# Merge gates and branch products by rows of tokens with transposed merged rows, and a hand-ordered tail in smaller pieces

## The chip, the core and the metric

One core of a Trainium2 chip runs the kernel alone. The metric is device microseconds (us) of one execution; the time before is 429.8 us, the median of three runs (429.72 to 430.73). The engines are TensorE (PE; its weight loads are listed apart as PEld), VectorE (DVE), ScalarE (ACT), GpSimd (POOL) and SyncE (SP), which here issues the loads of the weights and the stores of the output.

## The reference, cut to what matters

One decoder layer on 256 tokens of width 1024. Three attention mixers give `o_a`, `o_b` and `o_c` (together 1024 wide). Each is projected to 1024, the three are merged by sigmoid gates, and the merged rows go through `w_out`. A gated feed-forward part and a last RMS norm follow.

```python
gates = sigmoid(mg).reshape(b, s, 3, 1024)             # mg: 3072 columns of norm(x) @ w_in
merged = (gates[:, :, 0] * (o_a @ wb[:r0]) + gates[:, :, 1] * (o_b @ wb[r0:r1])
          + gates[:, :, 2] * (o_c @ wb[r1:]))
x = x + merged @ w_out
x = x + conv_ffn(rmsnorm(x, norm_ffn), w_up, conv_w, conv_b, w_down)
return rmsnorm(x, norm_final)
```

## The kernel before

All is float32. To keep its precision, each operand of the large products is cut into a high and a low part, and `mm3` (L239) makes three products of each: low by high, high by low, high by high. So one "product" of the mathematics is three instructions of TensorE, each with its own weight load.

**Weights.** `_unit_list` (L69) cuts all weights into units, most of 1 MB (2048 floats for each of 128 partitions), which SyncE loads in the order in which the program asks for them into `raw` buffers (4, and a fifth once the attention's memory is free). ACT copies a unit into its high part `whi` (L224), DVE subtracts to get the low part `wlo` (L228), each in two halves of 1024 floats. There are 2 buffers for such pairs, and 5 once the attention is done; a unit keeps its pair until its last product has been made.

**Order.** Outside of blocks marked `manual_schedule`, Tile's planner orders each engine's instructions ahead of time: what comes first in the program has priority, and where that isn't ready, something later that is ready is put in its place. On the chip each engine then keeps this order. PSUM tiles of a pool are taken when free: `psg` and, after the attention, `psg2` have two banks each, and `psa` has the four banks of the sums `acc[t][n]` (t: half of the tokens, n: half of the 1024 columns).

**Gates and branches, before.** Everything is computed transposed, with 128 output channels on the partitions and the 256 tokens along the free axis. `gates(i)` (L668) takes three units (one for each branch) of 256 gate columns; for each of two chunks of 128 columns `chunk_T` (L343) makes 24 instructions with the weights as the stationary operand and the 256 tokens moving, and ACT copies the 128x256 result into `gl`. There are 12 such units, i.e. 24 chunks and 576 instructions. The first two calls follow the attention in the program, so that their products are put into its holes; the other two are in the merge loop. The loop over four quarters of the columns (L725) loads `br{i}` and `wo{i}`, takes the sigmoid, and for each chunk makes the three branch products (9, 9 and 6 instructions with 256 moving columns), which DVE multiplies by the gates and adds up (L748 to L751) into `mg`. `mg` is already the transposed form that the product with `w_out` needs as its stationary operand; it is cut into `mh` (ACT, L754) and `ml` (DVE, L755).

`later` (L706) holds the products with `w_out` back: a chunk's 12 instructions of 512 columns are put in the program one chunk later (two at the end), so that TensorE need not wait for `mh` and `ml`. What is still held at the end is given out by `flush(t, n)` in the hand-ordered block that follows (L827), in which the sums are added to `x`, squared, transposed (L784) and split for the feed-forward part.

**The tail, before** (L946 to L960). The planner orders it. For each half t of the tokens: the last three chunks' products of the down projection, 9 instructions for each `acc[t][n]`; two adds of 512 columns, each followed by a sum of squares on ACT (L169); the rest of the norm (L178 on DVE, the power on POOL, L180); a product with the norm's weights (L953); a scaling of one half of the columns on DVE (L957) and one on ACT (L959); and two stores of 256 KB by SyncE (L960).

## Time and profile before

| | before |
|---|---|
| median of 3 runs | 429.80 us |
| the profiled execution | 429.01 us |
| span of its instructions | 427.2 us |
| TensorE busy | 417.7 us (98%) |
| DVE busy | 309.6 us (72%) |
| ACT busy | 253.6 us (59%) |
| mean granted TensorE clock | 0.995 |

The span runs from the first instruction to the last; the profiled execution took 1.8 us more than its span. A TensorE instruction's listed duration includes its passage through the array, which overlaps the next instruction's, so what a stream of products costs is the distance between the starts of two neighbours. The trace has three stages that matter here: the attention, until about 127 us; gates, branches and the product with `w_out`, from 127 to 234 us; and the tail, from about 413 us.

### The profile page before, as it was taken

The page shows a single profiled execution, that of the slowest core. Times are in us where ns is not written, and L with a number is a line of the kernel's source. Part 1 is how long each engine was busy: PE and PEld are TensorE (multiplying, and loading weights), DVE is VectorE, ACT ScalarE, POOL GpSimd, SP SyncE. Part 2 cuts the span into 40 slices and gives each one's busy share as a digit, 9 for nine tenths or more (in the row PEclk, how much of TensorE's full clock was granted, in tenths as well). Part 3 has the DMA queues.
Part 4 walks back from the last instruction along what each step waited for, and adds up shares of the span by engine and source line. Part 5 has one row for each costly group of instructions (what it writes and reads, how often), then busy time and mean ns, then how long its engine had stood idle before and what let it go on. Part 6 is the DMA issues. An engine that isn't in the chain of part 4 may idle for free.

```text
span 427.2 us, 7237 instructions
## 1 busy us (share of the span) xinstructions
PE 417.7 (98%) x2848; PEld 373.8 (87%) x2848; DVE 309.6 (72%) x641; ACT 253.6 (59%) x463; POOL 13.1 (3%) x19
## 2 busy tenths in 40 slices
PE   9999999999999999999999999999999999999993
PEld 8998888987779998999998998988888888888882
DVE  5756753798864697539345899998797797887764
ACT  6443282458787774445345889567576575584633
POOL 4201000000000000000000100000000000000001
PEclk9999999999999999999999999999999999999997
DMA  8988719532209785544540274665753743700002
GB/s 303 394 352 300 266 51 342 202 125 83 100 2 334 281 329 189 198 163 153 195 179 2 100 294 162 234 216 197 277 202 103 288 176 120 295 2 0 2 0 98
DMA packets 12609, 78.05 MB, mean 183 GB/s; under 512 B 1392, under 2 KB 1408, under 8 KB 4640
## 3 DMA queue, kind: packets, MB, share of 16 engines
q1 hardware_dynamic: 12000, 75.48, 47.5%
q0 software_dynamic: 576, 2.12, 1.6%
q8 instruction: 22, 0.36, 0.3%
q14 instruction: 11, 0.09, 0.1%
HBM read 76.52 MB, written 1.07 MB: 182 GB/s over the span
## 4 chain that ended last, share of the span: by engine, by line
PE 89%; ACT 4%; DVE 4%; issue 2%; POOL 0%; POOLq 0%; ACTq 0%
PE g L240 14%; PE g L242 13%; PE g L241 13%; PE g L924 12%; PE g L926 6%; PE acc L240 6%; PE acc L241 6%; PE acc L242 6%; PE o L489 2%; PE t L470 2%; PE g L824 2%; PE g L289 1%; PE s L456 1%; DVE cy L903 1%; PE g L882 1%
## 5 line engine op out<-in xcount | busy, mean ns | idle before, releaser
L228 DVE TENSOR_TENSOR wlo<-raw,whi 128x1024 fp32r<-128x1024 f32 (+2 forms) x130 | 153.9, 1204 | 48.4 <-ACT whi L224 47.7
L224 ACT ACTIVATE whi<-raw 128x1024 fp32r<-128x1024 f32 (+2 forms) x130 | 129.9, 1039 | 35.9 <-PE g L242 23.2
L240 PE MATMUL g<-hn_hi,wlo 128*128 128x256 f32 x376 | 108.2, 288 | 0.1
L241 PE MATMUL g<-hn_lo,whi 128*128 128x256 f32 x376 | 107.5, 286 | 0.0
L242 PE MATMUL g<-hn_hi,whi 128*128 128x256 f32 x376 | 107.2, 285 | 0.0
L924 PE MATMUL g<-parts,whi 128*128 128x512 f32 x256 | 89.4, 396 | 0.0
L240 PEld LDWEIGHTS g<-hn_hi,wlo 128*128 128x128 f32 x376 | 72.0, 191 | 2.9 <-issue 1.4
L242 PEld LDWEIGHTS g<-hn_hi,whi 128*128 128x128 f32 x376 | 72.0, 192 | 1.1 <-issue 1.0
L241 PEld LDWEIGHTS g<-hn_lo,whi 128*128 128x128 f32 x376 | 72.0, 192 | 0.7 <-issue 0.5
L926 PE MATMUL g<-parts,wlo 128*128 128x256 f32 x256 | 66.2, 279 | 0.0
L924 PEld LDWEIGHTS g<-parts,whi 128*128 128x128 f32 x256 | 46.7, 188 | 9.2
L926 PEld LDWEIGHTS g<-parts,wlo 128*128 128x128 f32 x256 | 48.2, 188 | 2.8
L903 DVE SCALAR_TENSOR_TENSOR cy<-xn,small_b,cy 128x255 f32<-128x255 f32 (+1 forms) x88 | 41.4, 478 | 8.9 <-ACT cy L901 8.0
L240 PE MATMUL acc<-whi,fl 128*128 128x512 f32 x88 | 34.5, 392 | 0.1
L241 PE MATMUL acc<-wlo,fh 128*128 128x512 f32 x88 | 34.3, 390 | 0.0
L242 PE MATMUL acc<-whi,fh 128*128 128x512 f32 x88 | 34.2, 389 | 0.0
L901 ACT ACTIVATE cy<-xn,small_b 128x256 f32<-128x256 f32 x44 | 25.8, 598 | 7.4 <-DVE xn L933 7.4
L932 ACT ACTIVATE xn<-g 128x256 f32<-128x256 f32 x32 | 12.2, 380 | 22.2 <-PE g L924 22.2
L674 ACT ACTIVATE gl<-g 128x256 f32<-128x256 f32 x24 | 9.1, 378 | 21.7 <-PE g L242 21.7
L242 PEld LDWEIGHTS acc<-whi,fh 128*128 128x128 f32 x88 | 16.5, 188 | 3.6
L933 DVE TENSOR_TENSOR xn<-g,xn 128x256 f32<-128x256 f32 x32 | 13.4, 420 | 8.4 <-ACT xn L932 8.4
L241 PEld LDWEIGHTS acc<-wlo,fh 128*128 128x128 f32 x88 | 16.5, 188 | 3.3
(190 smaller groups left out, 589.6 us busy)
## 6 DMA issues: line engine op xcount, KB each, us to landing
raw<-in_wts_dram SPq DMA_DIRECT2D x62, 1024.0 KB, 4.9
gl<-in_w_dram SPq DMA_DIRECT2D x8, 512.0 KB, 7.1
raw<-in_wts_dram SPq DMA_DIRECT2D x2, 804.0 KB, 7.5
raw<-in_wts_dram SPq DMA_DIRECT2D x3, 512.0 KB, 6.7
T<-tvd POOLq DMA_DIRECT2D x1, 1280.0 KB, 13.5
xs<-in_x_dram SPq DMA_DIRECT2D x2, 516.0 KB, 3.7
out_dram<-raw SPq DMA_DIRECT2D x4, 256.0 KB, 2.2
T<-tvd POOLq DMA_DIRECT2D x1, 768.0 KB, 7.7
```

What stands on the lines that cost most here:

```text
L224: nc.scalar.activation(self.parts[0][:, sl], self.raw[:, sl], AF.Copy)
L228: return (eng or nc.vector).tensor_sub(self.parts[1][:, sl], self.raw[:, sl], self.parts[0][:, sl].bitcast(F32))
L240: nc.tensor.matmul(ps, al, bh, start=start, stop=False)
L241: nc.tensor.matmul(ps, ah, bl, start=False, stop=False)
L242: nc.tensor.matmul(ps, ah, bh, start=False, stop=stop)
L674: nc.scalar.activation(gl[c][:, b, :], chunk_T(plain(u, c)), AF.Copy)
L901: on_act.append(nc.scalar.activation(y, u, AF.Identity, bias=vec_c[:, 3, ch:ch + 1], scale=vec_c[:, 2, ch:ch + 1]))
L903: nc.vector.scalar_tensor_tensor(y[:, sh:], u[:, :S - sh], vec_c[:, w, ch:ch + 1], y[:, sh:], op0=ALU.mult, op1=ALU.add)
L924: hi = lambda: nc.tensor.matmul(ps, u[0][:, k, cols], h_parts[:, k].rearrange("p a q -> p (a q)"), start=k == 0, stop=k == KC - 1)
L926: lo = lambda: nc.tensor.matmul(ps[:, :S], u[1][:, k, cols], h_parts[:, k, 0, :], start=False, stop=False)
L932: nc.scalar.activation(part, ps[:, S:], AF.Copy)
L933: nc.vector.tensor_add(v, ps[:, :S], part)
```

## The change

Gates and branch products are made by rows: 128 tokens on the partitions and 512 columns along the free axis. The activations become the stationary operand and the weights the moving one. The gates come from 12 units again, but each holds 512 rows by 512 columns; `by_rows` (the body of the former `proj_V`) makes 12 instructions of 512 columns for each half of the tokens and each unit, 288 in all. The branch products become 96 instructions of 512 columns in place of 192 of 256. They use `psg` alone, and the second half's gates use `psg2`. The merge runs in two halves of 512 columns in place of four quarters. The gates of one branch of a half are a tile of 128x1024, on which the sigmoid is taken at once; DVE multiplies in place and adds into `mg`, which now has tokens on the partitions. So 16 transposes on TensorE are new: eight per half, four into each bank. `mh` and `ml` are made from that bank, 128x512 at a time. The products with `w_out` are held back four chunks.

The tail gets a hand-written order. The last block of the sums, `acc[1][1]`, is given out as twice 9 instructions of 256 columns, the second of them into a bank of its own. The second token half is added in pieces of 512, 512 and 256 columns and squared in pieces of 512, 256 and 256, the last on DVE. Its second 512 columns get both factors of the norm in one DVE instruction. SyncE stores all, that part first. Single-use tiles of the norms get one buffer.

```diff
-    for i in range(4):
-        out += [(f"g{i}{b}", "w_in", rows, [(C_MG + D * b + 256 * i, 256)]) for b in range(3)]
-        out.append((f"br{i}", "w_branch", mixed, [(256 * i, 256)]))
-        out.append((f"wo{i}", "w_out", [(256 * i, 256)], [(0, D)]))
+    for n in range(2):
+        out += [(f"g{n}{b}{i}", "w_in", [(512 * i, 512)], [(C_MG + D * b + 512 * n, 512)]) for b in range(3) for i in range(2)]
+        out += [(f"br{n}{i}", "w_branch", mixed[i], [(512 * n, 512)]) for i in range(2)]
+        out += [(f"wo{i}", "w_out", [(256 * i, 256)], [(0, D)]) for i in (2 * n, 2 * n + 1)]
...
+    def by_rows(names, n, pool=psg):
+        pss = [pool.tile([P, 512], F32, name="g") for _ in range(NT)]
+        for i, name in enumerate(names):
+            u = unit(name)
             for t in range(NT):
                 for k in range(4):
                     kk = 4 * i + k
                     mm3(pss[t][:, :n], h_hi[:, kk, t * P:(t + 1) * P], h_lo[:, kk, t * P:(t + 1) * P],
                         u[0][:, k, :], u[1][:, k, :], kk == 0, kk == KC - 1)
+        return pss
...
-        gl = [pool.tile([P, 4, S], F32, name="gl", bufs=4)[:, 0:3, :] for _ in range(2)]
         for b in range(3):
-            u = unit(f"g{i}{b}")
-            for c in range(2):
-                nc.scalar.activation(gl[c][:, b, :], chunk_T(plain(u, c)), AF.Copy)
+            gl = mix.tile([P, 4, S], F32, name="gl", bufs=4) ...
+            pss = by_rows([f"g{n}{b}{i}" for i in range(2)], 512, pool)
+            for t in range(NT):
+                nc.scalar.activation(gl[:, t, :], pss[t], AF.Copy)
...
+    for n in range(2):
+        if n:
+            gl.append(gates(n, psg2))
+        br = [unit(f"br{n}{i}") for i in range(2)]
+        uo = [unit(f"wo{2 * n + i}") for i in range(2)]
...
+        for b in range(3):
+            nc.scalar.activation(gl[n][b], gl[n][b], AF.Sigmoid)
+        mg = [gl[n][0][:, t, :] for t in range(NT)]
+        for t in range(NT):
+            rows = slice(t * P, (t + 1) * P)
             for b, (k0, k1) in enumerate(branch_k):
-                ps = gtile()
+                ps = psg.tile([P, 512], F32, name="g")
                 for k in range(k0, k1):
+                    u = br[k // 4]
+                    mm3(ps, o_hi[:, k, rows], o_lo[:, k, rows], u[0][:, k % 4, :], u[1][:, k % 4, :], k == k0, k == k1 - 1)
+                nc.vector.tensor_mul(gl[n][b][:, t, :], ps, gl[n][b][:, t, :])
+                if b:
+                    nc.vector.tensor_add(mg[t], mg[t], gl[n][b][:, t, :])
+        for i in range(2):
+            ps = psg.tile([P, 512], F32, name="g")
+            for c in range(2):
+                for t in range(NT):
+                    nc.tensor.transpose(ps[:, c * S + t * P:c * S + (t + 1) * P], mg[t][:, (2 * i + c) * P:(2 * i + c + 1) * P], ident)
+            nc.scalar.activation(mh, ps, AF.Copy)
+            nc.vector.tensor_sub(ml, ps, mh.bitcast(F32))
+            for c in range(2):
+                later(acc, mh[:, c, :], ml[:, c, :], uo[i], c, dc == 0, dc == KC - 1, 4)
...
+    with tc.manual_schedule(engines={Activation, DVE, Pool, PE}):
+        for n in range(2):
+            flush(0, n)
+        ss = []
+        for n in range(2):
+            with_rest(0, n * 512, (n + 1) * 512)
+            ss.append(sum_of_squares(0, n * 512, (n + 1) * 512, f"z0{n}"))
+            weighted(0, n * 512, (n + 1) * 512)
+        r = rstd_of(ss, "z0")
+        flush(1, 0)
+        flush(1, 1, 0, 256)
+        own = bank()
+        flush(1, 1, 256, 512, own)
+        with_rest(1, 0, 512)
+        scaled_by_act(0, 0, nc.sync)
+        s0 = sum_of_squares(1, 0, 512, "z10")
+        weighted(1, 0, 512)
+        with_rest(1, 512, D)
+        s1 = sum_of_squares(1, 512, 768, "z11")
+        nc.scalar.activation(both, s0, AF.Identity, bias=s1)
+        scaled_by_act(0, 1, nc.sync)
+        nc.vector.tensor_add(xs[:, 1, 768:D], own[:, 256:512], xs[:, 1, 768:D])
+        nc.vector.tensor_tensor_reduce(y[:, 1, 768:D], xs[:, 1, 768:D], xs[:, 1, 768:D], ..., accum_out=s2)
+        nc.vector.tensor_scalar(ms, s2, both, EPS, op0=ALU.add, op1=ALU.add)
+        nc.gpsimd.tensor_tensor(r, ms, half, op=ALU.pow)
+        nc.vector.scalar_tensor_tensor(y[:, 1, 512:D], xs[:, 1, 512:D], r, gfin[:, 512:D], op0=ALU.mult, op1=ALU.mult)
+        store(nc.sync, 1, 512, D)
+        scaled_by_act(1, 0, nc.sync)
```

## Rows read from the trace of the kernel before

**Rows 1.** The page: busy time of each engine (share of the span) and its instructions; the granted clock in 40 slices of the span; the shares of the engines in the chain of work that ended last.

```profile
PE 417.7 (98%) x2848; PEld 373.8 (87%) x2848; DVE 309.6 (72%) x641; ACT 253.6 (59%) x463; POOL 13.1 (3%) x19
...
PEclk9999999999999999999999999999999999999997
...
PE 89%; ACT 4%; DVE 4%; issue 2%; POOL 0%; POOLq 0%; ACTq 0%
```

**Rows 2.** Busy time of TensorE in five stretches (start:end and length in us, busy time, instructions that lie in or reach into the stretch, granted clock, DMA share and GB/s). The first three are gates, the fourth is the branch products of the last quarter, the fifth products with `w_out`.

```profile
127.27:153.50 26.23, 26.23 (x220) 1.00 0.78 285
173.54:190.82 17.28, 17.28 (x146) 1.00 0.52 187
202.06:219.34 17.28, 17.28 (x146) 1.00 0.52 189
219.34:225.09 5.75, 5.75 (x50) 1.00 0.38 155
225.09:231.93 6.84, 6.84 (x32) 1.00 0.00 0
```

**Rows 3.** The time line of TensorE in a stretch of gates (start, duration, line, operation, shapes): ten instructions from the first to the last row, all of 256 moving columns.

```profile
139.96 0.28 PE L241 MATMUL g<-hn_lo,whi 128*128 128x256 f32 x1
140.08 0.28 PE L242 MATMUL g<-hn_hi,whi 128*128 128x256 f32 x1
140.20 0.28 PE L240 MATMUL g<-hn_hi,wlo 128*128 128x256 f32 x1
...
141.16 0.28 PE L242 MATMUL g<-hn_hi,whi 128*128 128x256 f32 x1
```

**Rows 4.** The same of a projection that is already made by rows (`proj_V`, L368), with 512 moving columns: 17 steps from the first to the last row.

```profile
36.06 0.39 PE L240 MATMUL g<-whi,hn_lo 128*128 128x512 f32 x1
36.28 0.39 PE L241 MATMUL g<-wlo,hn_hi 128*128 128x512 f32 x1
...
39.91 0.39 PE L242 MATMUL g<-whi,hn_hi 128*128 128x512 f32 x1
```

**Rows 5.** The chain that ended last, in order of time: the transposes of L784, eight in a row, twice.

```profile
232.10 0.87 PE acc L784 x8
...
236.26 0.87 PE acc L784 x8
```

**Rows 6.** Groups of instructions by line with shapes kept apart (count, busy us, mean ns of one, idle time before them and what ended it).

```profile
L228 DVE TENSOR_TENSOR wlo<-raw,whi 128x1024 fp32r<-128x1024 f32 x124 | 148.7, 1219 | 41.3 <-ACT whi L224 40.7
L224 ACT ACTIVATE whi<-raw 128x1024 fp32r<-128x1024 f32 x124 | 125.3, 1051 | 33.3 <-PE g L242 20.7 <-PE acc L242 9.6 <-DMA raw<-in_wts_dram 2.3
...
L903 DVE SCALAR_TENSOR_TENSOR cy<-xn,small_b,cy 128x255 f32<-128x255 f32 x44 | 20.9, 479 | 8.3 <-ACT cy L901 8.0
...
L942 ACT ACTIVATE fh<-sa 128x256 fp32r<-128x256 f32 x22 | 9.0, 408 | 5.7 <-DVE sa L939 5.6
...
L463 DVE CUSTOM_DVE_ANT_0 tt<-s,T 128x256 f32<-128x256 f32 x16 | 6.6, 415 | 0.0
L750 DVE TENSOR_TENSOR tmp<-g,gl 128x256 f32<-128x256 f32 x16 | 6.6, 420 | 1.1 <-PE g L242 0.6
...
L763 DVE TENSOR_TENSOR xs<-acc,xs 128x512 f32<-128x512 f32 x4 | 2.7, 687 | 1.3 <-PE acc L242 1.3
L953 DVE TENSOR_TENSOR raw<-xs,g 128x512 f32<-128x512 f32 x4 | 2.7, 684 | 0.8 <-ACT raw L169 0.8
L169 ACT ACTIVATE raw<-xs 128x512 f32<-128x512 f32 x4 | 2.5, 631 | 4.2 <-DVE xs L763 4.2
```

**Rows 7.** Busy time of all engines in the two merge stretches between gates, and in the last one (as in group 2, with PE, PEld, DVE, ACT and POOL).

```profile
153.50:173.54 20.04, 20.04 (x134) 18.45 (x133) 17.30 (x30) 10.69 (x14) 0.00 (x0) 1.00 0.62 234
190.82:202.06 11.24, 11.24 (x74) 10.27 (x73) 9.07 (x14) 7.33 (x9) 0.00 (x0) 1.00 0.49 182
219.34:231.93 12.59, 12.59 (x80) 11.35 (x79) 6.49 (x14) 5.18 (x9) 0.00 (x0) 1.00 0.17 71
```

**Rows 8.** The time line of the end of the merge: the last `mg`, `mh` and `ml`, products with `w_out` beside them, and ACT's copy of the next unit; in brackets the engine's idle time before and what ended it.

```profile
225.09 0.40 PE L240 MATMUL acc<-whi,ml 128*128 128x512 f32 x1
...
226.03 0.42 DVE L751 TENSOR_TENSOR mg<-mg,tmp 128x256 f32<-128x256 f32 x1
...
226.48 0.42 ACT L754 ACTIVATE mh<-mg 128x256 fp32r<-128x256 f32 x1 [2.47 <-DVE mg L751]
...
226.93 0.43 DVE L755 TENSOR_TENSOR ml<-mg,mh 128x256 fp32r<-128x256 f32 x1 [0.48 <-ACT mh L754]
...
228.04 2.01 ACT L224 ACTIVATE whi<-raw 128x1024 fp32r<-128x1024 f32 x2 [1.14 <-PE acc L242]
```

**Rows 9.** The time line of the end: from the first product of the last block `acc[1][1]` to the stores.

```profile
417.92 0.39 PE L240 MATMUL acc<-whi,fl 128*128 128x512 f32 x1
...
419.73 0.39 PE L242 MATMUL acc<-whi,fh 128*128 128x512 f32 x1
...
420.15 0.69 DVE L763 TENSOR_TENSOR xs<-acc,xs 128x512 f32<-128x512 f32 x1 [0.22 <-PE acc L242]
...
420.88 0.63 ACT L169 ACTIVATE raw<-xs 128x512 f32<-128x512 f32 x1 [0.19 <-DVE xs L763]
421.42 0.18 ACT L169 ACTIVATION_READ_ACCUMULATOR raw<-xs 128x1 f32 x1
421.64 0.21 DVE L178 TENSOR_SCALAR msz<-ssz,ssz 128x1 f32<-128x1 f32 x1 [0.19 <-ACT raw L169]
...
421.93 0.92 POOL L180 TENSOR_TENSOR rsz<-msz,half 128x1 f32<-128x1 f32 x1 [3.12 <-DVE msz L178]
422.89 0.72 ACT L959 ACTIVATE raw<-raw,rsz 128x512 f32<-128x512 f32 x1 [1.28 <-POOL rsz L180]
...
423.40 0.81 SPq L960 DMA_DIRECT2D out_dram<-raw  x2
```

More of the change, by code (lines that the diff above doesn't have):

```diff
@@ L166, in square_mean @@
     def square_mean(src, junk, tag):
-        ss = small.tile([P, 1], F32, name="ss" + tag)
+        ss = small.tile([P, 1], F32, name="ss" + tag, bufs=1)
         nc.scalar.activation(junk, src, AF.Square, scale=D ** -0.5, accum_out=ss)
@@ L172, in rstd_of @@
     def rstd_of(sums, tag):
-        ms = small.tile([P, 1], F32, name="ms" + tag)
+        ms = small.tile([P, 1], F32, name="ms" + tag, bufs=1)
         if len(sums) == 1:
@@ L178, in rstd_of @@
             nc.vector.tensor_scalar(ms, sums[0], sums[1], EPS, op0=ALU.add, op1=ALU.add)
-        r = small.tile([P, 1], F32, name="rs" + tag)
+        r = small.tile([P, 1], F32, name="rs" + tag, bufs=1)
         nc.gpsimd.tensor_tensor(r, ms, half, op=ALU.pow)
@@ L366, in plain @@
         return lambda part, k: u[part][:, k, c * P:(c + 1) * P]
-    def proj_V(unit_name, n, name):
-        v = qkv.tile([P, NT, n], F32, name=name)
-        pss = [psg.tile([P, 512], F32, name="g") for _ in range(NT)]
-        for i in range(2):
-            u = unit(f"{unit_name}{i}")
+    def by_rows(names, n, pool=psg):
+        pss = [pool.tile([P, 512], F32, name="g") for _ in range(NT)]
+        for i, name in enumerate(names):
+            u = unit(name)
             for t in range(NT):
@@ L377, in proj_V @@
                         u[0][:, k, :], u[1][:, k, :], kk == 0, kk == KC - 1)
+        return pss
+    def proj_V(unit_name, n, name):
+        v = qkv.tile([P, NT, n], F32, name=name)
+        pss = by_rows([f"{unit_name}{i}" for i in range(2)], n)
         for t in range(NT):
@@ L665, in decoder_layer, with gates @@
         put_o(po, 6 + j)
-    def gates(i, pool):
-        gl = [pool.tile([P, 4, S], F32, name="gl", bufs=4)[:, 0:3, :] for _ in range(2)]
+    def gates(n, pool=psg):
+        out = []
         for b in range(3):
-            u = unit(f"g{i}{b}")
-            for c in range(2):
-                nc.scalar.activation(gl[c][:, b, :], chunk_T(plain(u, c)), AF.Copy)
-        return gl
-    gl = {i: gates(i, mix) for i in range(2)}
+            gl = mix.tile([P, 4, S], F32, name="gl", bufs=4).rearrange("p a b -> p (a b)").rearrange("p (t n) -> p t n", t=NT)
+            pss = by_rows([f"g{n}{b}{i}" for i in range(2)], 512, pool)
+            for t in range(NT):
+                nc.scalar.activation(gl[:, t, :], pss[t], AF.Copy)
+            out.append(gl)
+        return out
+    gl = [gates(0)]
     mixer.close()
@@ L706, in later, with emit @@
     def later(acc, ah, al, w, c, start, stop, depth):
-        def emit(t, n):
-            mm3(acc[t][n], ah[:, t * P:(t + 1) * P], al[:, t * P:(t + 1) * P],
-                w[0][:, c, n * 512:(n + 1) * 512], w[1][:, c, n * 512:(n + 1) * 512], start, stop)
+        def emit(t, n, c0=0, c1=512, own=None):
+            cols = slice(n * 512 + c0, n * 512 + c1)
+            ps, first = (acc[t][n], start) if own is None else (own, waiting[0] is emit)
+            mm3(ps[:, c0:c1], ah[:, t * P:(t + 1) * P], al[:, t * P:(t + 1) * P],
+                w[0][:, c, cols], w[1][:, c, cols], first, stop)
         waiting.append(emit)
@@ L716, in later, with flush @@
                     e(t, n)
-    def flush(t, n):
+    def flush(t, n, *cols):
         for e in waiting:
-            e(t, n)
+            e(t, n, *cols)
     branch_k = ((0, 3), (3, 6), (6, 8))
     acc = sums()
-    for i in range(4):
-        if i not in gl:
-            gl[i] = gates(i, mix)
-        u = unit(f"br{i}")
-        uo = unit(f"wo{i}")
-        if i == 3:
+    for n in range(2):
[3 more added lines that the diff above has]
+        uo = [unit(f"wo{2 * n + i}") for i in range(2)]
+        if n:
             first = {"fa0": unit("fa0")}
@@ L946, in decoder_layer, with with_rest, weighted, store @@
     y = raw_tile().rearrange("p (t d) -> p t d", t=NT)
-    for t in range(NT):
+    def with_rest(t, a, b):
+        nc.vector.tensor_add(xs[:, t, a:b], acc[t][a // 512][:, a % 512:(b - 1) % 512 + 1], xs[:, t, a:b])
+    def weighted(t, a, b):
+        nc.vector.tensor_mul(y[:, t, a:b], xs[:, t, a:b], gfin[:, a:b])
+    def store(eng, t, a, b):
+        eng.dma_start(out[t * P:(t + 1) * P, a:b], y[:, t, a:b])
+    junk = mpool.tile([P, 512], F32, name="junk", bufs=1)
+    def sum_of_squares(t, a, b, tag):
+        return square_mean(xs[:, t, a:b], junk[:, 0:b - a], tag)
```

49 lines of the change are left out of this document (19 added, 30 removed).

## The prediction

> **What bounds the kernel now.** I read the page first. TensorE is busy 98% of the span and carries 89% of the chain that ended last; DVE and ACT are busy 72% and 59%; the granted clock is at its upper level, 2.4 GHz, in all but the last slice [rows 1]. So the question in each stage is how long TensorE's stream is. Next come the windows of the stages that change: in gates, branches and products with `w_out` TensorE has no idle time, and the clock is 1.00 [rows 2]. But busy time doesn't say what an instruction costs, since durations overlap; so I went to the time line and took the distance of starts. With 256 moving columns it is 1.20 us / 10 = 0.120 us (139.96 to 141.16, [rows 3]); with 512, in a projection that is already made by rows, 3.85 / 17 = 0.2265 us (36.06 to 39.91, [rows 4]). The windows agree: 144 products of gates fill 17.28 us (0.120), 30 products with `w_out` 6.84 us (0.228) [rows 2]. Columns alone would make the second twice the first; it is 1.89 times. Each instruction carries some 13 ns that don't depend on its columns, and the change halves the number of instructions for the same columns.
>
> **Gates.** 576 instructions of 256 columns become 288 of 512. Each pair saves 2 x 0.120 - 0.2265 = 0.0135 us. Of the first half's 288 old instructions, 218 run behind the attention, in the stretch from 127.27 us (the row's 220 less two of the attention's that reach into it), and 70 earlier, as filling of its holes [rows 2]. The 218 and the second half's 288 run back to back: 253 pairs x 0.0135 = 3.42 us saved. The 70 are 35 pairs, 0.47 us; where the attention and not TensorE sets the pace that is worth nothing. Bounds 0 and 0.47; I take 0.2. Loads and splits don't get in the way: a unit now lasts 24 x 0.2265 = 5.44 us instead of 48 x 0.120 = 5.76, against ACT's 2 x 1.05 and DVE's 2 x 1.22 us for one unit [rows 6]. At 1 MB in 5.44 us it asks for 193 GB/s, and the first stretch moved 285 [rows 2]. ACT's copies into `gl` go from 24 of 256 to 12 of 512; each has the other token half's 12 instructions, 2.7 us, to be done in.
>
> **Branches.** 192 instructions of 256 become 96 of 512: 96 x 0.0135 = 1.30 us saved. DVE's part shrinks: per half it was 4 chunks of 6 instructions at 0.42 us, 10.1 us; now it is 6 multiplications, 4 additions and 2 subtractions of 512 at 0.69 us, 8.3 us [rows 6].
>
> **Transposes.** 16 new ones. Eight in a row are 0.87 us of the chain, twice [rows 5]; 16 cost 1.74 us, all of it on TensorE. They may overlap a little more or, in runs of four, less: 1.6 to 1.9.
>
> **The hand-over** is the new wait. Before, `mg`, `mh` and `ml` of a chunk follow each other in 1.3 us (226.03 to 227.36) beside products already held back [rows 8]. Now, when a half's last branch product ends, TensorE needs: multiplication 0.69, addition 0.69, a run of transposes 0.44, `mh` about 0.63, `ml` 0.69: 3.1 us, with hand-offs some 3.4 [rows 5, 6]; transposes counted already, 3.0 are new. In the first half the next gates lie ready as cover (a unit is 5.44 us). In the second half no gates follow. There the cover is the first half's products with `w_out`, 4 x 12 x 0.228 = 10.9 us, held back until behind the first transposes. Part may be used up earlier: `wo0` and `wo1` keep two of five pairs of buffers meanwhile, so a later gate unit's split waits, and the planner fills that hole from these products. One hole is one unit's split, 1.05 + 1.22 = 2.3 us until its first half is there [rows 6]. ACT's copy at 228.04 waited for just such a product, so a pair is given back when its last product is done and not sooner [rows 8]. After one hole 8.6 us are left against 3.4. I take the hand-over at 0; uncovered it costs 3.0.
>
> **Banks.** Branch products now alternate over two banks instead of four. A group may start when the multiplication of the group before last is done. With DVE free that is 0.42 us from the start of its last product (419.73 to 420.15, [rows 9]) plus 0.69, less the product's own 0.23, so 0.88 us behind its end; the shortest group between lasts 6 x 0.2265 = 1.36. So 0, if DVE is no more than 0.48 us late. If late, gates of the second half, or held-back products, are there to fill.
>
> **The end of the merge.** `flush` gives out 12 instead of 6 instructions per block; their total is the same, and each add of 0.69 us has 2.7 us of cover instead of 1.4. Taken at 0; the cover is larger than before.
>
> **The tail.** Before: the last product starts at 419.73; its add 420.15; square 420.88; POOL's power 421.93; scaling 422.89; SyncE issues the last two stores from 423.40 [rows 9]. After, kept on the same clock: block `acc[1][1]` starts at 417.92 and takes 18 x 0.120 instead of 9 x 0.2265, so its last product starts at 419.96. A 256-column product is listed with 0.28 us instead of 0.39 [rows 3, 4], so the add starts about 0.31 later, 420.27. Add of 256, 0.42; DVE's square sum with its reading, 0.5 (L463's 0.415 and a short read); 0.21; hand-off 0.08 and power 0.92; hand-off 0.04; last DVE instruction, 512 columns, two factors. It is not in the trace: at least 0.68 (a plain multiplication, L953), at most twice L903's 0.479, 0.96; I take 0.479 and the 0.27 by which 512 exceed 256 columns, 0.75, since it is L903's operation [rows 6]. Sum: 420.27 + 0.42 + 0.5 + 0.21 + 1.0 + 0.04 + 0.75 = 423.2, 0.2 us earlier than 423.40 (bounds +0.05 and -0.3). ACT's last scaling, 0.72, ends beside it; its store stands behind the other in SyncE's queue, as before. SyncE's earlier stores and ACT's sums (0.63 + 0.19 for 512, some 0.6 for 256, 0.2 for their sum) end near 421.1, when DVE's square sum ends; ACT's scaling of the first token half comes after and is over by 421.9, before the power. The single buffers of the norms move nothing.
>
> **Sum.** -3.42 - 0.2 - 1.30 + 1.74 + 0 - 0.2 = -3.4 us on the profiled execution's 429.01, 425.6. That execution is 0.8 below the median of 429.80; on the median it is 426.4. For small waits that a changed order leaves I give back 0.1: 426.5 us, and a span near 423.9. With all bounds, 425.9 to 427.1.
>
> **A rule that speaks against it.** The trace shows 120 and 226.5 ns from start to start [rows 3, 4]. The Trainium skill, TensorE: Matmul & The Clock Gate, section Back-to-back issue gap, gives the gap of a warm matmul as its columns divided by 2.4 GHz plus some 2.5 ns, which would be 109 and 216 ns. By 2.5 ns a pair the change would save 0.96 us in place of 4.9 and come to about 430.4 us, an estimate. This trace disagrees: its fixed part is 13 ns.
>
> **Rivals.** (1) *The hand-over of the second half isn't covered*, because the held-back products were all spent in holes before. It costs 3.0 us: 429.5. Against it: only one hole of 2.3 us is certain. For it: all of them are ready early, and any other hole eats them too. (2) *DVE becomes the bound of the branch stage, on two banks*, which makes it slower. If each multiplication stands behind a split of 1.22 and an addition of 0.69, the bank comes free 2.8 us behind the group's end, 0.75 to 1.4 beyond the next group's 2.04 to 1.36; eight groups take back a bank, 6 to 11 us; unfilled that gives 432 to 438, half filled about 431. I name 432. It decides from 0.48 us of delay on. For it: DVE was busy 17.3 of 20.04 us in the first merge stretch; against it: 9.07 of 11.24 and 6.49 of 12.59 in the others, and TensorE had no gap in any [rows 7]. (3) *The pairs save nothing*, because with the activations as stationary operand a product of 512 takes as long as two of 256, 0.240: then 1.74 - 0.2 = +1.5 remains, 431.3. The projection's rows are of exactly the new form and show 0.2265, so this is nearly excluded [rows 4]. (4) *The attention's holes are filled better*: its order is drawn anew, and where it runs shorter by 1.5 us, 425.0.
>
> **How the numbers follow.** Forecast 0.67; (1) 0.15; (2) 0.10; (3) 0.02; (4) 0.06. A measurement of this kernel tells 0.3%, 1.3 us, from no change. Faster by more: forecast and (4), 0.73; within: (1), 0.15; slower: (2) and (3), 0.12. The range reaches from the better half of (4), 425.0, over the forecast's bounds to (1), 429.6; outside lie (2), (3) and part of (4), some 0.15.
>
> **What would show it right or wrong.** TensorE's instructions fall by 288 + 96 and rise by 16 + 9, to 2489. Right: starts 0.2265 us apart in gates and branches; some 3 us less from the attention's end (127.27 us) to the first transposes of L784 (231.93 us, the end of the fifth stretch) [rows 2]; no gap at the transposes of the second half, with products with `w_out` ahead of and between them; and from the first product of the last block to the first of the last two stores 5.3 us instead of 5.48 [rows 9]. Wrong: a gap of about 3 us there (1), waits on DVE's multiplication before branch products (2), or starts 0.24 apart (3).

## The result, and the profile after

The changed kernel took 426.95 us (median of 6, 426.29 to 427.72) against 430.22 for the kernel before beside it: ratio 0.9931, 95% interval 0.9917 to 0.9945. The forecast was 426.5. The same kernel was measured twice more, on two different chips (experiments 5 and 9): 0.994 and 0.9952. The first profiled execution took 426.73 us with a span of 424.9, before's 429.01 with 427.2; that pair differs by 2.3 us, the medians by 3.3, since before's profiled execution lay 1.2 below its median and after's 0.2.

The page after: busy time and instructions, granted clock, the shares of the chain, as in [rows 1].

```profile
PE 414.7 (98%) x2489; PEld 353.6 (83%) x2489; DVE 307.1 (72%) x618; ACT 251.6 (59%) x447; POOL 12.3 (3%) x19
...
PEclk9999999999999999999999999999999999999998
...
PE 83%; DVE 6%; ACT 5%; issue 2%; DMA 2%; POOL 1%; SPq 0%; POOLq 0%; ACTq 0%
```

TensorE has the predicted 2489 instructions and 3.0 us less of busy time. What is new stands in the chain: TensorE fell from 89 to 83%, and DMA, which [rows 1] do not list, is there with 2%. The time line of gates after the change answers to [rows 3], the windows of two stretches of gates and one of products with `w_out` to [rows 2] (start:end, length, busy time, instructions, clock, DMA share, GB/s).

```profile
152.15 0.39 PE L241 MATMUL g<-whi,hn_lo 128*128 128x512 f32 x1
152.38 0.39 PE L242 MATMUL g<-wlo,hn_hi 128*128 128x512 f32 x1
152.60 0.39 PE L243 MATMUL g<-whi,hn_hi 128*128 128x512 f32 x1
```

```profile
129.30:153.50 24.20, 24.20 (x110) 1.00 0.76 280
168.70:181.00 12.30, 12.30 (x56) 1.00 0.67 254
218.10:228.80 10.70, 10.70 (x50) 1.00 0.11 44
```

Starts are 0.23 us apart and TensorE has no idle time there. The hand-over of the second half, where the prediction saw its main risk, on the time line:

```profile
216.40 0.40 PE L241 MATMUL acc<-whi,ml 128*128 128x512 f32 x1
216.45 0.69 DVE L758 TENSOR_TENSOR gl<-gl 128x512 f32<-128x512 f32 x1
...
216.63 0.27 PE L764 MATMUL g<-ident,gl 128*128 128x128 f32 x1
...
216.66 0.47 PE L242 MATMUL acc<-wlo,mh 128*128 128x512 f32 x1
...
216.97 0.39 PE L243 MATMUL acc<-whi,mh 128*128 128x512 f32 x1
...
217.20 0.39 PE L241 MATMUL acc<-whi,ml 128*128 128x512 f32 x1
...
217.43 0.82 PE L764 MATMUL g<-ident,gl 128*128 128x128 f32 x6
217.95 0.60 ACT L769 ACTIVATE mh<-g 128x512 fp32r<-128x512 f32 x1 [4.33 <-PE g L764]
```

While DVE makes the last addition (216.45), products held back run on TensorE, and the transposes slip in between them: no gap. The tail, from the first product of the last block to the last two stores, answers to [rows 9]:

```profile
416.11 0.28 PE L241 MATMUL acc<-whi,fl 128*128 128x256 f32 x1
...
418.14 0.28 PE L243 MATMUL g<-whi,fh 128*128 128x256 f32 x1
...
418.46 0.42 DVE L1006 TENSOR_TENSOR xs<-g,xs 128x256 f32<-128x256 f32 x1
...
418.92 0.42 DVE L1008 CUSTOM_DVE_ANT_0 raw<-xs 128x256 f32<-128x256 f32 x1
...
419.46 0.21 DVE L1011 TENSOR_SCALAR msz<-ssz,ssz 128x1 f32<-128x1 f32 x1
419.75 0.55 POOL L1013 TENSOR_TENSOR rsz<-msz,half 128x1 f32<-128x1 f32 x1 [3.09 <-DVE msz L1011]
...
420.33 0.75 DVE L1014 SCALAR_TENSOR_TENSOR raw<-xs,rsz,g 128x512 f32<-128x512 f32 x1 [0.66 <-POOL rsz L1013]
```

```profile
421.11 0.81 SPq L971 DMA_DIRECT2D out_dram<-raw  x2
```

From 416.11 to 421.11 it is 5.00 us; before it was 5.48, predicted 5.3. GpSimd's power takes 0.55 us; before it was 0.92.

**Where the time went.** I added up the distances from start to start on TensorE's time line, by kind of instruction, from the last transpose ahead of the first product of attention weights with V (60.08 us before, 60.74 after) to the first FFN product (234.18 and 232.38):

| | predicted | before | after | measured |
|---|---|---|---|---|
| gates and other products with `hn` of 256 and 512 columns | -3.62 | 91.30 | 87.57 | -3.73 |
| branch products | -1.30 | 23.17 | 21.90 | -1.27 |
| new transposes | +1.74 | | 1.39 | +1.39 |
| the attention's transposes, with the waits at them | 0 | 5.00 | 5.99 | +0.99 |
| products with `w_out`, the rest | 0 | 54.63 | 54.78 | +0.15 |
| whole stretch | -3.2 | 174.10 | 171.64 | -2.46 |

The tail adds -0.48, and the changed kernel's run came to the stretch 0.66 us later (its first weights landed later: first conversion 8.63 against 7.79 us). -2.46 - 0.48 + 0.66 = -2.28, the difference of the two spans.

Two of these rows can't be read by themselves. Behind a transpose the next product's step, from its start to that of the one after it, is some 0.09 us longer: 216.66 to 216.97 above is 0.31 where 0.23 is usual. With these steps, which stand in the rows of the products, the 16 transposes cost 1.39 + 0.53 = 1.92 us. And the -3.73 includes what 41 gate products save in the attention's holes, while the waits that they bring there stand in the fourth row (experiment 7).

Below, "excess" of a stretch is the sum of these distances less 226.7, 120, 183 or 110 ns for each instruction of 512, 256, 402 or fewer columns. Only its differences mean something. From the attention's last product with V to the first transposes of L784 (L801 after), "the merge" for short, it was 0.60 us before and 0.96 after. A "stop" is a single distance that is over 0.25 us too long.

### The profile page after: what moved, and what is told of

Read it like the earlier page. It is cut to its first block, busy times and chain, and to the rows that moved or that the text cites. A ratio compares the mean times of both kernels' runs of the same rounds, so it can differ in the third digit from the quotient of the medians.

```text
span 424.9 us, 6471 instructions
## 1 busy us (share of the span) xinstructions
PE 414.7 (98%) x2489; PEld 353.6 (83%) x2489; DVE 307.1 (72%) x618; ACT 251.6 (59%) x447; POOL 12.3 (3%) x19
## 4 chain that ended last, share of the span: by engine, by line
PE 83%; DVE 6%; ACT 5%; issue 2%; DMA 2%; POOL 1%; SPq 0%; POOLq 0%; ACTq 0%
PE g L241 13%; PE g L243 13%; PE g L242 13%; PE g L941 12%; PE g L943 6%; PE acc L241 6%; PE acc L242 6%; PE acc L243 6%; PE g L841 2%; DVE wlo L229 2%; DMA raw<-in_wts_dram 2%; PE t L476 2%; PE o L495 1%; ACT tt L513 1%; DVE cy L920 1%
## 5 line engine op out<-in xcount | busy, mean ns | idle before, releaser
L241 PE MATMUL g<-hn_hi,wlo 128*128 128x256 f32 x184 | 53.3, 290 | 0.1
L243 PE MATMUL g<-hn_hi,whi 128*128 128x256 f32 x184 | 52.6, 286 | 0.0
L242 PE MATMUL g<-hn_lo,whi 128*128 128x256 f32 x184 | 52.3, 284 | 0.0
L242 PE MATMUL g<-wlo,hn_hi 128*128 128x512 f32 (+1 forms) x128 | 50.0, 391 | 0.0
L243 PE MATMUL g<-whi,hn_hi 128*128 128x512 f32 (+1 forms) x128 | 49.8, 389 | 0.0
L241 PE MATMUL g<-whi,hn_lo 128*128 128x512 f32 (+1 forms) x128 | 49.6, 389 | 0.0
L241 PEld LDWEIGHTS g<-hn_hi,wlo 128*128 128x128 f32 x184 | 35.2, 191 | 2.7 <-issue 1.4
L243 PEld LDWEIGHTS g<-hn_hi,whi 128*128 128x128 f32 x184 | 35.2, 191 | 1.0 <-issue 0.8
L242 PEld LDWEIGHTS g<-hn_lo,whi 128*128 128x128 f32 x184 | 35.2, 191 | 0.2
L241 PE MATMUL acc<-whi,fl 128*128 128x512 f32 (+1 forms) x88 | 34.2, 389 | 0.1
```

Source lines behind the costliest of these rows:

```text
L241: nc.tensor.matmul(ps, al, bh, start=start, stop=False)
L242: nc.tensor.matmul(ps, ah, bl, start=False, stop=False)
L243: nc.tensor.matmul(ps, ah, bh, start=False, stop=stop)
```

## The experiments

Theories: the merge by rows saves 13 ns for each pair of instructions, less the transposes, and the held-back products cover the hand-over; the tail saves 0.5 us since GpSimd's power is no longer slowed. Rivals: the gain is from the tail or from elsewhere; the cover isn't needed; the power was shorter for another reason.

**1. The merge without the tail**: before's tail put back.

```diff
-        flush(1, 1, 0, 256)
-        own = bank()
-        flush(1, 1, 256, 512, own)
...
+    for t in range(NT):
+        for n in range(2):
+            flush(t, n)
+        r = add_back(t, y[:, t, :], "z")
...
```

> The changed kernel with the old tail. My theory (the merge's gain is fewer instructions of TensorE): 2.5 to 3.2 us faster than the kernel before (ratio 0.9926 to 0.9942), the merge stretch as in the changed kernel, and POOL's last power again 0.92 us long, as the old tail has DVE multiply beside it. Rival (a large part of the gain is the tail's): only about 1.5 us faster (0.9965).

Measured: 428.94 us (427.68 to 430.52), ratio 0.998, interval 0.9966 to 0.9994. Both expectations missed it. Its instructions stand in the same order on each engine as the changed kernel's up to the tail, so the loss isn't the merge's order. ScalarE's time line shows where about half of it is:

```profile
149.61 0.60 ACT L681 ACTIVATE gl<-g 128x512 f32<-128x512 f32 x1 [0.18 <-PE g L243]
153.00 2.00 ACT L225 ACTIVATE whi<-raw 128x1024 fp32r<-128x1024 f32 x2 [2.79 <-DMA raw<-in_wts_dram]
154.91 0.58 ACT L681 ACTIVATE gl<-g 128x512 f32<-128x512 f32 x1
```

A conversion of weights waits 2.79 us for its load, and the evacuation of finished gates (ScalarE's copy out of their PSUM bank) stands behind it in ScalarE's order; TensorE needs that bank and stops for 1.36 us at 154 us. The changed kernel's first profile has the same conversion at 151.19, after 0.28 us of waiting, and no stop. The excess of the merge is 3.56 us here against 0.96. Of the 2.6 us between them the stop is 1.36; about 1.0 is spread over the products from 155 us on, which are some ns slower each, for a reason that no run tells (last section). POOL's last power took 0.92 us, as expected.

**2. The tail without the merge**: the kernel before with these lines the other way round.

```diff
-    def flush(t, n):
+    def flush(t, n, *cols):
...
+        flush(1, 1, 0, 256)
+        own = bank()
+        flush(1, 1, 256, 512, own)
...
```

> The kernel before with the new tail alone. Prediction's term: 0.2 us faster (ratio 0.9995). Theory after the changed kernel's profile: 0.5 us faster (0.9988), because POOL's power takes 0.55 us instead of 0.92 when DVE does nothing beside it; the profile shows the power at 0.55. Rival (the stores end the run, and their time is the same): 0 to 0.1 us.

Measured: 429.50 (428.62 to 430.05), ratio 0.9988 (0.9979 to 0.9998): -0.5 us, as the profile of the tail has it: the last power takes 0.55 us, and from the first product of the last block to the first of the last two stores it is 5.00. The merge in it is before's, and its profile has stops too, of 0.29 and 0.98 us (waits of 156 to 164 us: total, times, longest):

```profile
PEld g L240 <- DVE mg L750: 1.0, 1, 1.0
PE g L240 <- DVE mg L750: 0.8, 1, 0.8
```

Here the multiplication stands behind VectorE's half of a conversion that ran late, since ScalarE had waited 1.46 us for the load of the one ahead of it; before's profile has the same order without that wait. The excess of the merge is 1.92 where before's profile has 0.60. So late loads strike both kernels.

**3. Nothing held back in the first half.**

```diff
-                later(acc, mh[:, c, :], ml[:, c, :], uo[i], c, dc == 0, dc == KC - 1, 4)
+                later(acc, mh[:, c, :], ml[:, c, :], uo[i], c, dc == 0, dc == KC - 1, 0 if n == 0 else 4)
```

> The changed kernel, but the first half's products with w_out are no longer held back: they stand in the program right behind their transposes, so none is left as cover when the second half's merged rows are turned. Theory (held-back products cover the hand-over): TensorE waits about 3.0 us at the second half's transposes, and the run is about 3 us longer than the changed kernel, near the kernel before (ratio 0.999 to 1.001). Rival (the planner finds other cover, or the hand-over is short): no gap over 1 us there, ratio 0.993 to 0.995.

Measured: 431.31 (429.53 to 432.62), ratio 1.0027 (1.0012 to 1.0042), slower than before. The waits of 219 to 225 us:

```profile
PE acc L241 <- DVE ml L770: 1.1, 1, 1.1
...
PE g L764 <- DVE gl L756: 0.7, 1, 0.7
...
PE g L764 <- DVE gl L758: 0.4, 1, 0.4
```

From start to start these are 0.84, 0.62 and 1.25 us more than the instructions need, 2.7 in all (the prediction had 3.0 for it), and 0.71 us more are lost at 212.6 us, where a branch product waits for a bank. Without the held-back products the change is no gain.

**4. Branch products in pieces of 256 columns**, still by rows, in four banks.

```diff
-                ps = psg.tile([P, 512], F32, name="g")
+                for j in range(2):
+                    cols = slice(256 * j, 256 * (j + 1))
+                    ps = bank()[:, :256]
...
```

> The changed kernel with each branch product of 512 columns made as two of 256 in banks of their own (192 instructions instead of 96; the multiplications by the gates are cut as well; stationary operand and columns the same). Theory (a fixed cost per instruction): starts 0.120 us apart, 1.3 us longer than the changed kernel (ratio 0.996). Rival (the gain comes from the exchange of stationary and moving operand, not from the size): starts 0.113 us apart, ratio 0.993, no change.

Measured: 428.97 (427.78 to 431.71), ratio 0.9983 (0.9966 to 1.0). The profile has a late load's stop of 1.1 us at 157.3; without that distance the branch products are 120.4 ns apart on average, against 228.1 for 512 columns in the changed kernel. 2 x 120.4 - 228.1 = 12.7 ns, times 96 pairs 1.2 us: the term was 1.30. The total can't tell, as the changed kernel has no run on record on this chip. By the gap that the Trainium skill, TensorE: Matmul & The Clock Gate, section Back-to-back issue gap, gives for an isolated warm matmul it would be 96 x 2.5 ns = 0.24 us, an estimate; the trace disagrees. The same section says that in a stream of weight loads and matmuls both set the spacing, so its formula, which the prediction set against its own sum, was not meant for such a stream.

**5. The changed kernel again, on another chip.**

> The changed kernel itself, once more, beside the three below. In the profiles so far one load of weights, the 26th of the 67 on SyncE's queue (the first of w_out), took 5.1 us from its issue to its first conversion in the changed kernel, but 7.6 us with the merge alone and with the tail alone; behind it stands an evacuation of gates on ScalarE (or the branch's multiplication on VectorE), and TensorE stood 1.55 and 1.27 us there, and not at all in the changed kernel's profile. Theory (this arrival differs from run to run and from chip to chip, and is no part of the change): the ratio to the kernel before is 0.995 to 0.998 where the load is late as it was for the merge alone, and the profile then shows the same stop near 154 us; near 0.993 where it isn't. Rival (the merge without the tail is really worth only 0.998, and the tail is worth the rest): 0.993 here too, with no stop.

Measured: 426.88 (426.27 to 428.58), ratio 0.994 (0.9919 to 0.9962). The load of question took 5.6 us to land (7.6 in experiment 1), and TensorE has no stop. By itself this fits theory and rival; number 9 decides.

**6. w_out's conversions on GpSimd** (first half).

```diff
...
+                if n == 0:
...
+                    nc.gpsimd.tensor_copy(u.parts[0][:, sl], u.raw[:, sl])
+                    u.lo(j, 2, nc.gpsimd)
...
```

> The changed kernel, with both halves of the first two units of w_out (loads 26 and 27) converted on GpSimd instead of ScalarE and VectorE, so that a late load holds up nothing that TensorE waits for: their first product is some 20 us later. Theory of the late load: no stop of TensorE over 0.2 us between 150 and 160 us, a narrower scatter of the times, and a ratio of 0.992 to 0.994 whatever the unaltered kernel beside it shows, so 1 to 1.5 us under it where that has the stop. Rival 1 (the scatter is from elsewhere): the same time as the unaltered kernel within 0.3 us. Rival 2 (GpSimd's conversions, 2.4 us for each quarter of the first weights, slow VectorE's beside them or come too late for w_out's products): 0.5 to 2 us more than the unaltered kernel, with VectorE's conversions longer than 1.2 us or a stop before the first products with w_out.

Measured: 430.28 (428.95 to 431.13), ratio 1.0006, 3.4 us over number 5 on the same chip. Rival 2 it was, with more than the 2 us that it gave at most. I had also named the wrong load: the late one stayed on ScalarE here, so it isn't w_out's; the semaphores that the conversions wait for, and the buffer that each load reuses, make it the first unit of the second half's gates. The groups of 148 to 164 us, and windows of all engines:

```profile
L229 POOL TENSOR_TENSOR wlo<-raw,whi 128x1024 fp32r<-128x1024 f32 x4 | 11.9, 2991 | 0.0
L229 DVE TENSOR_TENSOR wlo<-raw,whi 128x1024 fp32r<-128x1024 f32 x4 | 10.1, 2586 | 2.6 <-ACT whi L225 2.6
```

```profile
156.00:160.00 4.00, 1.68 (x8) 1.08 (x7) 3.96 (x5) 0.00 (x0) 4.00 (x2) 1.00 1.01 426
160.00:164.00 4.00, 4.00 (x12) 3.11 (x12) 3.91 (x3) 0.00 (x0) 3.40 (x2) 0.57 0.65 262
```

VectorE's conversion takes 2.59 us beside GpSimd's where it takes 1.22 alone [rows 6]. The branch's multiplications come late, TensorE stops for 2.5 us at 156.3, and in the window after that the granted clock is 0.57, with products 0.43 us apart.

**7. A finer filler in the attention**: the first gates of the first half in pieces of 256 columns.

```diff
+            if n == 0 and b == 0:
+                us = [unit(f"g{n}{b}{i}") for i in range(2)]
+                for j in range(2):
+                    cols = slice(256 * j, 256 * (j + 1))
+                    pss = [pool.tile([P, 512], F32, name="g")[:, :256] for _ in range(NT)]
...
```

> The changed kernel, with the first branch's gates of the first half made in pieces of 256 columns (48 pairs of products in place of 48 single ones, +0.65 us by 13.5 ns each), the pieces that fill the attention's waits. Theory (a coarser filler costs the attention: TensorE's excess before and after the attention's transposes rose from 5.0 to 6.0 us): this falls back to 5.0 to 5.3 us, and the run ends 0.1 to 0.4 us under the unaltered kernel. Rival (the order was only drawn anew, the size of the filler has no part in it): the excess stays at 6.0 us or is anything else, and the run is 0.6 us longer.

Measured: 427.28 (426.49 to 428.23), ratio 0.9941, against 426.88 for number 5 on the same chip. The attention's transposes went back from 6.02 to 5.03 us, as the theory had it, but that isn't the whole account: the excess of all of the attention (first to last product with V) is 0.54 us higher in the changed kernel than before, and 0.24 higher here. The 0.54 is just what the coarse filler saves by its size: 41 products of 512 columns run in the attention, and 41 x 13.3 ns = 0.55 us. The starts themselves say the same. From the first product with V to the first gate product behind the last one it was 66.99 us before (60.28 to 127.27, [rows 2]); in the changed kernel it is 68.41, from 60.94 to this row:

```profile
129.35 0.50 PE L243 MATMUL g<-whi,hn_hi 128*128 128x512 f32 x1
```

That is 1.42 us more, for gates worth 82 instructions of 256 columns in place of 70, 12 x 0.120 = 1.44 us. So the coarse filler neither gains nor loses in the attention. The finer one gives back 0.30 us of waits and gives up the 0.55: for the same work the attention is 0.25 us longer with it.

**8. VectorE's multiplication beside the last power.**

```diff
-        weighted(1, 0, 512)
         with_rest(1, 512, D)
...
         nc.gpsimd.tensor_tensor(r, ms, half, op=ALU.pow)
+        weighted(1, 0, 512)
```

> The changed kernel, with VectorE's multiplication of 128x512 by the final norm's weights, of the last tokens, put beside GpSimd's last power instead of ahead of the last addition. Theory (GpSimd's power takes 0.92 us in place of 0.55 because VectorE works on two operands beside it): the last power takes 0.9 us again, the multiplication starts about when the power does, and from the first product of the last block to the first of the last stores it is 5.3 to 5.4 us in place of 5.00. Rival (the power was shorter for another reason, such as a smaller wait or its operands' place): 0.55 us still, and 5.0 to 5.2 us. The total moves by under 0.4 us either way, which the timed runs can hardly show.

Measured: 427.98 (426.48 to 429.31), ratio 0.9953. The time line of the end:

```profile
420.78 0.68 DVE L968 TENSOR_TENSOR raw<-xs,g 128x512 f32<-128x512 f32 x1
420.94 0.92 POOL L1012 TENSOR_TENSOR rsz<-msz,half 128x1 f32<-128x1 f32 x1 [3.10 <-DVE msz L1010]
```

0.92 us again, beside a multiplication that began 0.16 us earlier. From the first product of the last block to the first of the last two stores it is 5.38 us in place of 5.00. This settles the power. The Trainium skill, SBUF — State Buffer, section Who interferes with whom, says that a DVE instruction with two inputs in SBUF contends with a GpSimd instruction that reads SBUF; these rows and those of number 6 agree. The run is 1.1 us longer than number 5, which the tail alone doesn't explain: its profile also has a stop of 0.56 us at 142 us.

**9. The unaltered changed kernel once more, and three edits of the late loads, on one chip.**

> The changed kernel, unaltered, as the measure for the three below on the same chip. By the theory of late loads its times lie between 426.3 us (no stop) and some 430 us (a stop of 1 to 3 us between the attention's end and the transposes), by how fast the loads between 123 and 160 us land on this chip; the ratio to the kernel before is 0.992 to 0.998. Rival (no such thing): 0.993 to 0.994 again, whatever the loads take.

Measured: 428.32 (427.36 to 429.1), ratio 0.9952 (0.9935 to 0.997). Its profile has two stops, 0.63 us at 141.9 and 0.88 at 155.6. ScalarE's time line:

```profile
138.32 3.90 ACT L225 ACTIVATE whi<-raw 128x1024 fp32r<-128x1024 f32 x4 [2.01 <-DMA raw<-in_wts_dram]
142.13 1.06 ACT L681 ACTIVATE gl<-g 128x512 f32<-128x512 f32 x2
...
154.15 2.01 ACT L225 ACTIVATE whi<-raw 128x1024 fp32r<-128x1024 f32 x2 [1.98 <-DMA raw<-in_wts_dram]
156.07 0.58 ACT L681 ACTIVATE gl<-g 128x512 f32<-128x512 f32 x1
```

The same instructions in the same order, and twice an evacuation behind a conversion that waits for DMA. The profiles thus speak against the rival (0.993 to 0.994 whatever the loads take); the timed runs alone don't exclude it, since the interval begins at 0.9935.

**10. The final norm's weights loaded after the merge.** The load moves behind the merge, with a one-column copy that makes it wait; order on TensorE, ScalarE and GpSimd unchanged.

```diff
-    nc.sync.dma_start(gfin, norms[0:1, :].to_broadcast([P, D]))
...
+    nc.vector.tensor_copy(gfin[:, 0:1], xs[:, 0, 0:1])
+    nc.sync.dma_start(gfin, norms[0:1, :].to_broadcast([P, D]))
     y = raw_tile().rearrange("p (t d) -> p t d", t=NT)
```

> The changed kernel, with the load of the final norm's weights (512 KB, on SyncE's queue at 129.5 us, where it waits for the attention's memory and then lands beside the 22nd load of weights) held back until the merge is done; on TensorE, ScalarE and GpSimd the order of instructions is the same. Theory: the 22nd load, for whose landing ScalarE's conversions and the gates' evacuation behind them wait (8.1 us with a stop of 0.56 us at 142 us in one run, 6.5 us without a stop in others), takes 4.8 to 5.2 us; no stop near 142 us; the median is 0 to 0.6 us under the unaltered kernel beside it. Rival (the loads are late for want of bandwidth of the whole stretch, or their lateness has nothing to do with that load): the same time within 0.3 us, or a later load as late as before.

Measured: 427.45 (426.64 to 428.63), ratio 0.9943 (0.9925 to 0.9961), 0.87 us under number 9; the intervals overlap. The 22nd load from issue to landing, first in number 9, then here:

```profile
DMA to landing us min/median/max: 8.1/8.1/8.1
```

```profile
DMA to landing us min/median/max: 4.9/4.9/4.9
```

In number 12, which has this edit too, that load takes 4.8 us; in the nine other profiles with this order of loads it takes 6.5 to 8.1, and the three with 8.0 or 8.1 are those with a stop at 142 us. That stop is gone here, as expected, and the one at 154 us is there (0.80).

**11. The late load's conversion put behind the gates' last evacuation**: its scale is a 1.0 made from the first branch product.

```diff
...
+                if (n, t, b) == (0, 0, 0):
+                    one.append(small.tile([P, 1], F32, name="one", bufs=1))
+                    nc.vector.tensor_scalar(one[0], gl[n][b][:, t, 0:1], 0.0, 1.0, op0=ALU.mult, op1=ALU.add)
...
```

> The changed kernel, with the conversion of the second half's first gate weights made to wait for the first branch product's multiplication (its scale is a 1.0 that VectorE makes from that product), so that it stands behind the gates' last evacuation on ScalarE and no longer ahead of it. By the semaphores that the conversions wait for, and by the run with w_out's conversions on GpSimd, in which it stayed on ScalarE, the late 26th load is this one, and not w_out's as was written for that run. Theory: no stop of TensorE over 0.2 us between 150 and 160 us, however late that load is; a median 0.3 to 1.5 us under the unaltered kernel if that one has the stop here, the same within 0.3 us if not; highest and lowest time less far apart. Rival (the load's lateness only shifts the stop to the first products that use these weights, or VectorE's conversions now collide with the branch's multiplications): the stop is found between 160 and 170 us instead, with the same or a longer time.

Measured: 428.51 (428.04 to 429.69), ratio 0.9965. The stop behind the evacuation is gone, but TensorE stops for 0.65 us at 156.9 instead, behind the next conversion, now on VectorE (and for 0.52 at 141.2, as in number 9). ScalarE's time line, then VectorE's:

```profile
153.16 0.60 ACT L683 ACTIVATE gl<-g 128x512 f32<-128x512 f32 x1 [1.83 <-PE g L245]
153.65 2.00 ACT L225 ACTIVATE whi<-raw 128x1024 fp32r<-128x1024 f32 x2
```

```profile
154.74 2.36 DVE L229 TENSOR_TENSOR wlo<-raw,whi 128x1024 fp32r<-128x1024 f32 x2 [2.07 <-ACT whi L225]
157.01 1.28 DVE L758 TENSOR_TENSOR gl<-g,gl 128x512 f32<-128x512 f32 x2
```

So the stop only moved by one engine, as the rival said, though earlier than it said. And it no longer hangs on a load: ScalarE's half of that conversion waits for no DMA here, it follows the evacuation at once. What delays the multiplication is the order that the edit brought.

**12. Both edits**, the diffs of numbers 10 and 11 together.

> Both of these edits in the changed kernel. Theory: neither stop, 425.9 to 426.9 us on any chip, and the narrowest scatter of the four. Rival (the scatter of the times is not from these two stops): the scatter of the unaltered kernel, and a median within 0.3 us of it.

Measured: 428.34 (428.17 to 428.84), ratio 0.9961. The scatter is the narrowest of the four, 0.67 us against 1.74 in number 9, but at a time no better: the stop of 0.65 us on VectorE is in its profile too, and, as in number 11, the products of the merge are some ns slower from 155 us on, about 1.2 us in all (last section). The theory is at most half right: with six runs each, it is likely but not shown that the scatter comes from these loads, and in place of them the edit of number 11 brings a stop of its own. No version tried is shown to beat the changed kernel on all chips.

## Why the prediction was right, and where its steps were not

- **Bound and pitch**: right. 2489 instructions, 0.227 us apart; gates -3.73 in place of -3.62, branches -1.27 in place of -1.30 (13 ns a pair by experiment 4). Rival 3, pairs that save nothing, is excluded. That the gates' row comes out so near is partly luck: it holds 0.55 us saved in the attention's holes, which were lost again beside it.
- **Transposes**: right in kind, a little short: 1.92 us in place of 1.74, with bounds of 1.6 to 1.9. Up to the start of the next product the 16 take 1.39, but that product's own step is then longer (216.63, 216.66 and 216.97 above).
- **Hand-over** at 0: right, with the cover that was named. Without the cover 2.7 us and a bank's 0.7 (experiment 3), where 3.0 had been said. Rival 1 did not come about, and one change of depth makes it come.
- **Banks** at 0: right where loads land in time. Rival 2, 6 to 11 us, didn't come; but its mechanism, a multiplication behind a conversion, is what stops TensorE in experiments 2, 11 and 12, by 0.65 to 1.3 us, in experiment 2 with four banks.
- **The 35 pairs in the attention's holes**: 0 in place of -0.2, the end of the stated bounds at which they are worth nothing. The 41 products that ran there save 0.55 us by their size and bring 0.54 us of waits (experiment 7); 0.30 of these went again with a filler half as long, the rest is the new order or not told apart. Rival 4 didn't come about: for the same work the attention took as long as before.
- **Tail**: -0.48 in place of -0.2. The mis-sized term is the power: 0.92 was taken from a row in which VectorE multiplied beside it; alone it takes 0.55 (419.75 above; experiment 8 brings the 0.92 back). Every other term was within 0.1.
- **Small waits, and "loads and splits don't get in the way"**: the step that failed. +0.1 was given back. In a profile without a stop the excess rose by 0.36 (0.96 - 0.60), of which 0.16 are the transposes, counted there at 0.110 each; in others it rose by up to 3.0 (3.56 - 0.60 in experiment 1, 1.36 of it the stop and about 1.0 slower products). The argument was by rates, 193 GB/s wanted where 285 had been moved. But one and the same load took 6.5 to 8.1 us in runs with the same order of loads (experiment 10), and its conversion stands in order ahead of an evacuation or multiplication that TensorE needs at once. Both kernels have this, and it is part of why profiled executions differ by more than the tail is worth.
- **A mark ill chosen**: 3 us less up to the first transposes of L784 came out as 3.16 (231.93 to 228.77), yet the first FFN product moved by 1.80 only, because six more held-back products per block stand behind that mark. Counted from the attention's end, as the mark says, it is even 5.2 us (127.27 to 231.93, 129.35 to 228.77), since six more gate products of 512 columns ran ahead of that end.

On the profiled execution the forecast was 425.7 with the 0.1 for waits, and 426.73 was measured: the stretch of the table came out 0.72 higher than its terms (-2.46 for -3.18: 0.2 in the attention, 0.2 at the transposes, some 0.3 of small waits and of pairs that moved into the attention) and the run came to it 0.66 later, while the tail gave 0.28 more and the 0.1 was already counted. On the median it was 426.5 against 426.95. There the later start is within the scatter: in the profiles with the changed kernel's attention the first product with V starts between 60.24 and 61.17 us. What stays open: the merge and the tail alone are worth 0.2% and 0.12% in the timed runs, together 0.5 to 0.7%; the profile of the merge's run puts the difference on a late load's stop and on slower products, but the changed kernel has no run on record on that chip.

## What to carry to other kernels

Where TensorE is full, count instructions, not columns only: on this trace half as many instructions for the same columns saved 13 ns a pair, provided that work held back covers the new dependency. In the attention's holes the same pairs saved nothing: the longer pieces overran by as much. When an instruction's cost is read from distances of starts, look at the step behind it too: part of a transpose's cost stood in the next product's. Before a load is called hidden, look at what stands behind its consumer in that engine's order, and take a second profile: one execution may have a stop of 1 us that another lacks.

## What the runs showed of the hardware

- GpSimd and VectorE slowed each other when a VectorE instruction with two inputs ran beside GpSimd: a power of 128x1 took 0.92 in place of 0.55 us, a conversion on VectorE 2.59 in place of 1.22.
- A transpose of 128x128 between products of 512 columns cost some 0.12 us (1.92 for 16), partly in the step of the product behind it; eight in a row are 0.109 us apart.
- After a stop of 2.5 us in experiment 6 the granted clock of the next window was 0.57 on average, that is the lower level of 1.2 GHz for most of it, with products of 512 columns 0.43 us apart; after stops of 0.6 to 1.4 us it stayed at 1.00, the upper level.
- In the profiles of experiments 1, 11 and 12 products of 512 columns were mostly 231 to 236 ns apart between 186 and 202 us (median 233), in the other profiles with such products the median was 227 or 228, at a granted clock of 1.00 in both. Summed from the attention's end to the transposes of L801, distances within 25 ns of the nominal ones give 1.3 to 1.5 us of excess there and 0.2 to 0.35 in the other profiles of merges by rows. Why, no run tells; experiment 1 has the same order of instructions as the changed kernel.
